# A decoder layer on one core: weight sums handed out one unit later in the plan, and the second down factor split during the last up product

## The chip, the cores and the metric

The kernel runs on one core of a Trainium2 chip. The metric is the device time of one execution in microseconds, measured on that core. The kernel before took a median of 954.35 us over three runs (953.08 to 955.14 us).

## What is computed

One layer of a decoder trunk, for 512 tokens of width 1024, all in float32: retention and dilated attention side by side, their gated sum, a feed-forward block, and a gated embedding. The parts that the change touches are the branch gates and the feed-forward block:

```python
h = rmsnorm(x, g_mix)
z = h @ w_in                                   # the last 2048 columns are the gates gl
gate_r, gate_a = split(sigmoid(gl + b_gate), 2)
x = x + (gate_r * ret_branch + gate_a * att_branch) @ w_o
u = rmsnorm(x, g_mlp) @ w_up                   # 1024 -> 4096
x = x + square(relu(u)) @ w_down               # 4096 -> 1024
```

## The kernel before

**Precision.** Every matrix product is made of three TensorE matmuls (lines 262 to 264, `mm3`): each float32 factor is split into a high part, a copy that ScalarE rounds, and a low part, the difference that VectorE forms. For weights the two instructions are in `split_unit`: the copy to `whi` at line 250 and the subtraction to `wlo` at line 251. For activations they are in `slots`: lines 1300 (copy) and 1301 (subtraction) to a tile `f`.

**Seven products.** Large products are done with seven half-size products in place of eight. Product 1 uses the weight block B11, product 5 uses T1, product 2 uses B21, product 3 uses B22, products 6, 7 and 4 use T2, T3 and T4. T1 is the sum of two blocks of weights, one of which is B11 (stored with the sign that the scheme wants). A product has two halves along its contraction, and one half of one weight block is a *unit*: a 128x1024 float32 tile, loaded in one transfer of 512 KB, split once, and read by 24 matmuls of 256 columns (up and gate products, where the weights are the stationary side) or 12 matmuls of 512 columns (down products). `HALVES` gives the order of units for gates, up and down products; it has 12 entries and 14 units:

```python
SEVEN = ((1, 0), (5, 0), (1, 1), (5, 1), (2, 0), (3, 0), (3, 1), (6, 0), (6, 1), (2, 1), (7, None), (4, None))
HALVES = ((1, 0), (1, 1), (5, 0), (5, 1)) + SEVEN[4:]
```

So in `HALVES` units 0 and 1 are B11, units 2 and 3 are T1, unit 4 is the first half of B21, units 5 and 6 are B22, units 7 and 8 are T2, unit 9 is the second half of B21, 10 and 11 are T3, 12 and 13 are T4.

**The plan of weights.** `make_plan` lists all units of the kernel in order. `plan_seven` adds the fourteen of one product. With "T1" in `vector`, T1's raw tile is loaded with one of its two blocks, and VectorE adds B11's raw tile to it (line 226); this is noted in `self.added` under the unit at which it is to be handed out. T2, T3 and T4 reuse a raw tile of an earlier unit: as soon as that unit is split, GpSimd issues an accumulating transfer into it (line 228), noted in `self.chained`. `ahead` walks the plan: it fetches a unit (line 212, on SP), splits it, then does the sum and the accumulating transfer noted under it. `units` is called before each product or half and runs `ahead` two units past what it hands out (`AHEAD`), three in the stages with a fixed order, until the first result of the stage sets it back to two. There are six raw tiles, and four tiles each for `whi` and `wlo`.

**Order on the engines.** In most of the kernel the tile framework's scheduler orders the instructions of each engine from their dependencies and the order in which the program traces them. Inside `manual_schedule` (the product with `w_o`, and everything from the last down product on) ScalarE and VectorE keep the traced order of the instructions inside.

**Feed-forward.** The loop at the end of `tail` runs four times: `up_products` (1024 columns of `w_up`) and then `seven_gemm` on 1024 rows of `w_down`, seven products each. When an up product has ended, `after` evacuates it (line 1323), combines it with an earlier one (line 1325), applies relu and square on ScalarE (lines 1326 and 1327) and forms the seven left factors of the down product: differences on VectorE (lines 1332, 1334 and 1306), then a split (lines 1300 and 1301) in two parts, p = 0 and p = 1. Factors 1 and 5 are split in `after`; the splits of the others are put in the dictionary `before` under the entry of the down product's `HALVES` ahead of which they are traced. The down product's results are added to the residual `x` on VectorE (line 1286).

Of the kernel before, what the change touches and what calls it, by code (L numbers as in the profile page):

```python
# [36 lines left out]
HALVES = ((1, 0), (1, 1), (5, 0), (5, 1)) + SEVEN[4:]  # L37
# [38 lines left out]
def R(ap):  # L76
    return ap.bitcast(F32R)


class Block:  # L80
# [90 lines left out]
    def plan_seven(self, w, r0, c1, c2, order, vector=()):  # L171

        cols = (c1, c2)
        q = lambda i, j, u: w[r0 + 512 * i + 256 * u : r0 + 512 * i + 256 * (u + 1), cols[j] : cols[j] + 512]
        n = len(self.plan)
        units = [(FACTOR[m], v) for m, u in order for v in ((0, 1) if u is None else (u,))]
        at = lambda name, u: n + units.index((name, u))
        for name, u in units:
            if name == "T1":
                src = q(0, 1, u) if name in vector else (q(0, 1, u), q(0, 0, u))  # L180
                if name in vector:
                    self.added[at("B11", u)] = at("T1", u), at("B11", u)
            elif name == "T4" and name in vector:
                self.added[max(at("B21", u), at("T2", u))] = at("T2", u), at("B21", u)
                src = (None, at("T2", u))
            elif name[0] == "B":
                src = q(int(name[1]) - 1, int(name[2]) - 1, u)
            else:
                prev, ij = {"T2": ("T1", (1, 1)), "T3": ("B22", (0, 1)), "T4": ("T2", (1, 0))}[name]
                k = at(prev, u)  # L190
                self.chained[k] = q(*ij, u)
                src = (None, k)
            self.plan.append((src, None))
# [1114 lines left out]
    def up_products(self, h2):  # L1308

        nc = self.nc  # L1310
        U, split = self.slots()
        held, before = {}, {}
        v = lambda ap: ap.rearrange("p (k t) -> p k t", k=2)

        def after(m, p, ps):
            k = slice(2 * p, 2 * p + 2)
            if m in (1, 3, 5):
                held[m, p] = self.tmp("r") if m != 5 else self.tabp.tile([P, 512], F32, tag="tab", name=self.nm("r5"))
                nc.scalar.activation(held[m, p], ps, AF.Copy)
                return  # L1320
            x = self.tmp("r4") if m == 4 else held[{2: 1, 6: 3, 7: 5}[m], p]
            if m == 4:
                nc.scalar.activation(x, ps, AF.Relu)
            else:
                nc.vector.tensor_tensor(x, x, ps, op=ALU.add)
                nc.scalar.activation(x, x, AF.Relu, scale=1.0 if m == 2 else -1.0)
            nc.scalar.activation(x, x, AF.Square)
            a11, a12, a21 = held.get((3, p)), held[1, p], held[5, p]
            if m == 6:
                split(1, v(a11), k)  # L1330
            elif m == 7:
                nc.vector.tensor_tensor(a11, a11, a21, op=ALU.subtract)
            elif m == 4:
                nc.vector.tensor_tensor(a21, x, a21, op=ALU.subtract)
                split(5, v(a21), k)
                self.differ(a21, x, a11)
                s3 = self.tmp("r3")
                rest = lambda m, a: lambda: split(m, v(a), k)
                third = lambda: self.differ(s3, a12, a21)
                for i, fn in ((p, third), (5 * p, rest(2, a12)), (1 + p, rest(3, s3)), (4 + p, rest(6, a21)),  # L1340
                              (7 + p, rest(7, a11)), (9 + p, rest(4, x))):
                    before.setdefault(i, []).append(fn)

        self.seven_products(lambda m, kk: (R(h2[m][:, 0, kk]), R(h2[m][:, 1, kk])), after, HALVES, "cb")
        return U, before


# [169 lines left out]
```

## Time and profile before

| | |
|---|---|
| median of three runs | 954.35 us (953.08 to 955.14) |
| the profiled execution | 955.36 us |
| its span, first to last instruction | 953.6 us |
| TensorE busy | 943.3 us (99%), 5357 matmuls |
| VectorE busy | 718.4 us (75%) |
| ScalarE busy | 562.1 us (59%) |
| GpSimd busy | 159.5 us (17%) |
| mean granted clock of TensorE | 0.997 |

The profile is of one execution. PE is TensorE's matmul, PEld its weight load, DVE is VectorE, ACT is ScalarE, POOL is GpSimd, SP is SyncE; L251 is line 251 of the kernel. Times run from the start of the span. The end of a matmul is modelled, so its start times are the firmer ones. Releasers are inferred from semaphores. The four up products begin near 587, 665, 744 and 822 us and the four down products near 627, 706, 784 and 863 us.

### The profile page before, as it was taken

The numbers are of one execution on the slowest core, as the hardware profiler recorded it, in microseconds if no ns is written. First come the engines' busy times: TensorE is split into PE (matmuls) and PEld (weight loads), VectorE is DVE, ScalarE is ACT, GpSimd is POOL, SyncE is SP. The second block draws the span as 40 slices with busy tenths as digits, with TensorE's granted clock in tenths as the row PEclk, the third lists the DMA queues.
The fourth block names the chain that finished last, engine by engine and source line by source line (L and its number), as shares of the span: only waits on it lengthen the run. The fifth ranks groups of instructions, "written<-read, shape, count | busy, mean of one in ns | idle before, by whom it ended". The sixth has DMA issues, their size and how long they took to land.

```text
span 953.6 us, 14325 instructions
## 1 busy us (share of the span) xinstructions
PE 943.3 (99%) x5357; PEld 826.2 (87%) x5357; DVE 718.4 (75%) x997; ACT 562.1 (59%) x1065; POOL 159.5 (17%) x140
## 2 busy tenths in 40 slices
PE   9999999999899999999999999999999999999998
PEld 6888888888788888999988888988998998998887
DVE  7789964766697849386937889799499689769953
ACT  5657775445745566576714446884494486467651
POOL 0322210222001112223012211111212302112100
PEclk9999999999999999999999999999999999999999
DMA  9953466258437645869737677868958968876911
GB/s 333 282 170 82 106 141 215 64 118 195 148 111 155 173 100 138 163 181 217 232 115 236 148 178 214 206 153 222 199 156 202 191 183 157 224 172 159 288 50 56
DMA packets 92549, 162.87 MB, mean 171 GB/s; under 512 B 8608, under 2 KB 20544, under 8 KB 92480
## 3 DMA queue, kind: packets, MB, share of 16 engines
q1 hardware_dynamic: 65168, 113.37, 36.4%
q0 software_dynamic: 23936, 46.14, 29.0%
q10 hardware_dynamic: 3376, 2.44, 0.9%
q8 instruction: 42, 0.69, 0.3%
q14 instruction: 27, 0.22, 0.1%
HBM read 153.49 MB, written 6.34 MB: 168 GB/s over the span
## 4 chain that ended last, share of the span: by engine, by line
PE 92%; DVE 3%; ACT 1%; issue 1%; DMA 1%; POOL 1%; SPq 0%; ACTq 0%; POOLq 0%; DVEq 0%
PE pg L264 25%; PE pg L262 25%; PE pg L263 25%; PE pa L264 3%; PE pa L263 3%; PE pa L262 3%; PE po L835 1%; PE ph L590 1%; DVE wlo L251 1%; PE pe L694 1%; PE sc L787 1%; PE ry L1083 1%; PE kv L1070 1%; PE ry L1085 1%; DVE ro L578 0%
## 5 line engine op out<-in xcount | busy, mean ns | idle before, releaser
L251 DVE TENSOR_TENSOR wlo<-raw,whi 128x1024 fp32r<-128x1024 f32 (+1 forms) x258 | 306.8, 1198 | 112.7 <-ACT whi L250 111.8
L250 ACT ACTIVATE whi<-raw 128x1024 fp32r<-128x1024 f32 (+1 forms) x257 | 266.3, 1041 | 212.1 <-PE pg L264 87.2
L263 PE MATMUL pg<-f,whi 128*128 128x256 f32 x384 | 108.7, 283 | 0.0
L264 PE MATMUL pg<-f,wlo 128*128 128x256 f32 x384 | 108.7, 283 | 0.0
L262 PE MATMUL pg<-f,whi 128*128 128x256 f32 x384 | 108.7, 283 | 0.0
L262 PE MATMUL pg<-whi,hh 128*128 128x512 f32 x248 | 98.6, 398 | 0.0
L264 PE MATMUL pg<-whi,hl 128*128 128x512 f32 x248 | 97.1, 392 | 0.0
L263 PE MATMUL pg<-wlo,hh 128*128 128x512 f32 x248 | 96.8, 390 | 0.0
L262 PE MATMUL pg<-whi,f 128*128 128x512 f32 x192 | 75.4, 393 | 0.0
L263 PE MATMUL pg<-wlo,f 128*128 128x512 f32 x192 | 74.8, 389 | 0.0
L264 PE MATMUL pg<-whi,f 128*128 128x512 f32 x192 | 74.8, 389 | 0.0
L262 PEld LDWEIGHTS pg<-f,whi 128*128 128x128 f32 x384 | 73.7, 192 | 0.2
L263 PEld LDWEIGHTS pg<-f,whi 128*128 128x128 f32 x384 | 73.7, 192 | 0.2
L264 PEld LDWEIGHTS pg<-f,wlo 128*128 128x128 f32 x384 | 73.7, 192 | 0.0
L228 POOL DMA_DIRECT2D raw<-in_w_in x32 | 38.9, 1216 | 197.8 <-DVE wlo L251 193.0
L264 PEld LDWEIGHTS pg<-whi,hl 128*128 128x128 f32 x248 | 46.6, 188 | 9.8
L263 PEld LDWEIGHTS pg<-wlo,hh 128*128 128x128 f32 x248 | 46.6, 188 | 9.2
L262 PEld LDWEIGHTS pg<-whi,hh 128*128 128x128 f32 x248 | 46.6, 188 | 9.2
L228 POOL DMA_DIRECT2D raw<-in_w_down x24 | 29.0, 1215 | 139.3 <-DVE wlo L251 108.2
L262 PE MATMUL pg<-whi,us 128*128 128x512 f32 x128 | 52.1, 407 | 0.0
L228 POOL DMA_DIRECT2D raw<-in_w_up x24 | 29.0, 1211 | 135.0 <-DVE wlo L251 124.7
L264 PE MATMUL pg<-whi,us 128*128 128x512 f32 x128 | 50.0, 391 | 0.0
(280 smaller groups left out, 2298.0 us busy)
## 6 DMA issues: line engine op xcount, KB each, us to landing
raw<-in_w_in SPq DMA_DIRECT2D x72, 512.0 KB, 4.1
raw<-in_w_in POOLq DMA_DIRECT2D x32, 512.0 KB, 6.2
raw<-in_w_up SPq DMA_DIRECT2D x32, 512.0 KB, 4.6
raw<-in_w_down SPq DMA_DIRECT2D x32, 512.0 KB, 4.6
raw<-in_w_up POOLq DMA_DIRECT2D x24, 512.0 KB, 6.6
raw<-in_w_down POOLq DMA_DIRECT2D x24, 512.0 KB, 5.9
x<-in_x SPq DMA_DIRECT2D x8, 512.0 KB, 8.2
raw<-in_w_ret_out SPq DMA_DIRECT2D x8, 512.0 KB, 3.8
```

The lines of the kernel that those rows point to most:

```text
L228: self.nc.gpsimd.dma_start(raw, self.chained[i].rearrange("(k p) n -> p k n", p=P), accum_op=ALU.add)
L250: self.pin(nc.scalar.activation(R(hi[:, i]), raw[:, i], AF.Copy))
L251: nc.vector.tensor_tensor(R(lo[:, i]), raw[:, i], hi[:, i], op=ALU.subtract)
L262: t.matmul(ps, sh, mh, start=first, stop=False, skip_group_check=more)
L263: t.matmul(ps, sh, ml, start=False, stop=False, skip_group_check=more)
L264: t.matmul(ps, sl, mh, start=False, stop=last, skip_group_check=more)
L590: self.nc.tensor.transpose(ps[:, t * P : (t + 1) * P], rots[t][:, h * HD : (h + 1) * HD], self.ident)
L694: self.nc.tensor.transpose(ps[:, k * P : (k + 1) * P], e[:, k * P : (k + 1) * P], self.ident)
L787: nc.tensor.matmul(sc[:, h * P : (h + 1) * P], qT[:, h, rs], kT[:, h, rs], start=True, stop=True)
L835: nc.tensor.matmul(po[:, h * P : (h + 1) * P], v[:, vt, h * HD : (h + 1) * HD], pt, start=b == 0, stop=b == len(blocks) - 1)
L1070: nc.tensor.matmul(ps, kd[:, n, hs], v[:, n, c], start=True, stop=True)
L1083: nc.tensor.matmul(y, sT[0][:, r], v[:, i, c], start=True, stop=i == 0)
```

## The change

In `plan_seven`, the vector sum of T1 is noted under the unit ahead of T1's own, no longer under B11's. With `HALVES` the sum for unit 2 is then handed out after unit 1 is split (before: after unit 0), and the sum for unit 3 after unit 2 is split (before: after unit 1). With `SEVEN` the unit ahead of T1's is B11's, and nothing changes.

In `up_products`, the split of the second left factor of the following down product leaves `before` (entries 0 and 5 of the down product) and is traced ahead of entry 11 of the up product, its last one, through a new dictionary `own` that is handed to `seven_products`.

```diff
@@ -179,7 +179,7 @@
             if name == "T1":
                 src = q(0, 1, u) if name in vector else (q(0, 1, u), q(0, 0, u))
                 if name in vector:
-                    self.added[at("B11", u)] = at("T1", u), at("B11", u)
+                    self.added[at("T1", u) - 1] = at("T1", u), at("B11", u)
@@ -1309,7 +1309,7 @@
         U, split = self.slots()
-        held, before = {}, {}
+        held, before, own = {}, {}, {}
@@ -1326,7 +1326,9 @@
             a11, a12, a21 = held.get((3, p)), held[1, p], held[5, p]
-            if m == 6:
+            if m == 2:
+                own.setdefault(11, []).append(lambda: split(2, v(x), k))
+            elif m == 6:
                 split(1, v(a11), k)
@@ -1337,11 +1339,11 @@
-                for i, fn in ((p, third), (5 * p, rest(2, a12)), (1 + p, rest(3, s3)), (4 + p, rest(6, a21)),
+                for i, fn in ((p, third), (1 + p, rest(3, s3)), (4 + p, rest(6, a21)),
                               (7 + p, rest(7, a11)), (9 + p, rest(4, x))):
                     before.setdefault(i, []).append(fn)
 
-        self.seven_products(lambda m, kk: (R(h2[m][:, 0, kk]), R(h2[m][:, 1, kk])), after, HALVES, "cb")
+        self.seven_products(lambda m, kk: (R(h2[m][:, 0, kk]), R(h2[m][:, 1, kk])), after, HALVES, "cb", own)
         return U, before
```

## Rows read from the trace of the kernel before

**Rows 1.** The page, busy time (share of span) and instructions of each engine

```profile
PE 943.3 (99%) x5357; PEld 826.2 (87%) x5357; DVE 718.4 (75%) x997; ACT 562.1 (59%) x1065; POOL 159.5 (17%) x140
```

**Rows 2.** Waits of PE, whole span: total us, times, longest

```profile
PE pc L884 <- DVE wide L878: 3.0, 1, 3.0
...
PE sc L795 <- DVE sm L678: 0.8, 1, 0.8
```

**Rows 3.** Stretches: length, busy us (count) by engine, clock, DMA share, GB/s

```profile
665.00:706.00 41.00, 41.00 (x340) 40.88 (x340) 26.74 (x29) 27.07 (x38) 7.25 (x6) 1.00 0.77 184
706.00:744.00 38.00, 38.00 (x168) 31.05 (x168) 36.80 (x47) 21.40 (x28) 7.25 (x6) 1.00 0.82 190
863.00:903.00 40.00, 40.00 (x187) 32.90 (x186) 38.69 (x55) 26.91 (x43) 8.83 (x8) 1.00 0.84 210
587.00:903.00 316.00, 316.00 (x2036) 288.72 (x2035) 262.69 (x320) 205.98 (x291) 59.61 (x50) 1.00 0.82 193
```

**Rows 4.** Waits of TensorE's weight loads from 587 to 930 us

```profile
PEld pg L262 <- DVE x L1286: 0.3, 1, 0.3
```

**Rows 5.** Line 226 (ns min/median/max); the page's DMA issues of down weights

```profile
L226 DVE TENSOR_TENSOR raw<-raw,raw x32: 1214/1218/1227, 56.9 to 854.8; 128x1024 f32<-128x1024 f32 x32
...
raw<-in_w_down SPq DMA_DIRECT2D x32, 512.0 KB, 4.6
```

**Rows 6.** Timeline (start, us, what), second gate product: VectorE, then TensorE

```profile
423.75 2.35 DVE L251 TENSOR_TENSOR wlo<-raw,whi 128x1024 fp32r<-128x1024 f32 x2
...
427.99 0.36 PE L262 MATMUL pg<-hh,whi 128*128 128x256 f32 x1
```

**Rows 7.** Timeline of VectorE, last up to last down product

```profile
854.82 1.22 DVE L226 TENSOR_TENSOR raw<-raw,raw 128x1024 f32<-128x1024 f32 x1
...
862.01 0.69 DVE L1334 TENSOR_TENSOR r<-r,r 128x512 f32<-128x512 f32 x1 [0.17 <-ACT r L1327]
863.40 0.69 DVE L1301 TENSOR_TENSOR f<-r,f 128x512 fp32r<-128x512 f32 x1 [0.70 <-ACT f L1300]
...
865.46 0.68 DVE L1301 TENSOR_TENSOR f<-r,f 128x512 fp32r<-128x512 f32 x1
...
866.66 1.22 DVE L251 TENSOR_TENSOR wlo<-raw,whi 128x1024 fp32r<-128x1024 f32 x1
...
875.53 1.40 DVE L1286 SCALAR_TENSOR_TENSOR x<-pg,f,x 128x512 f32<-128x512 f32 x2
...
879.79 2.35 DVE L251 TENSOR_TENSOR wlo<-raw,whi 128x1024 fp32r<-128x1024 f32 x2
```

**Rows 8.** Timeline of VectorE, second up to second down product

```profile
706.81 1.28 DVE L1301 TENSOR_TENSOR f<-r,f 128x512 fp32r<-128x512 f32 x2
...
714.68 2.35 DVE L251 TENSOR_TENSOR wlo<-raw,whi 128x1024 fp32r<-128x1024 f32 x2
...
720.61 0.68 DVE L1301 TENSOR_TENSOR f<-r,f 128x512 fp32r<-128x512 f32 x1
```

**Rows 9.** Timeline of TensorE: unit 4 (second down); units 2, 5 (last)

```profile
716.74 0.39 PE L263 MATMUL pa<-wlo,f 128*128 128x512 f32 x1
...
868.40 0.39 PE L263 MATMUL pg<-wlo,f 128*128 128x512 f32 x1
...
876.42 0.47 PE L262 MATMUL pg<-whi,f 128*128 128x512 f32 x1
```

**Rows 10.** Timeline of ScalarE, last up to last down product

```profile
860.73 0.58 ACT L1323 ACTIVATE r<-pg 128x512 f32<-128x512 f32 x1
...
862.73 1.15 ACT L1300 ACTIVATE f<-r 128x512 fp32r<-128x512 f32 x2 [0.76 <-DVE r L1334]
...
877.20 1.06 ACT L250 ACTIVATE whi<-raw 128x1024 fp32r<-128x1024 f32 x1 [0.70 <-DMA raw<-in_w_down]
```

**Rows 11.** Stretches behind the two waits of TensorE, columns as in rows 3

```profile
110.00:120.00 10.00, 10.00 (x50) 8.36 (x49) 8.52 (x18) 9.50 (x30) 1.20 (x1) 1.00 0.69 150
256.00:260.00 4.00, 3.89 (x16) 3.09 (x17) 0.00 (x0) 4.00 (x15) 0.00 (x0) 0.59 0.64 244
```

## The prediction

> **What bounds the kernel now.** I read four views in this order. First the busy shares of the page: TensorE is busy for 943.3 of 953.6 us, VectorE for 718.4 and ScalarE for 562.1 [rows 1]. A busy TensorE may still be one that waits inside modelled ends, so second comes what TensorE waited for: over the whole kernel there are two waits of note, 3.0 us for `wide` (line 878) and 0.8 us for `sm` (line 678) [rows 2], both long before the stages that this change touches. The third view is the busy time by stage. From 587 to 903 us, which is nearly all of the four up and down products, TensorE is busy for every one of 316 us; the only wait of its weight loads there that concerns this change is 0.3 us on VectorE's update of `x` (line 1286) [rows 3, 4]. An up product (665 to 706) has VectorE at 26.7 of 41 us; a down product (706 to 744) has it at 36.8 of 38, and the last one (863 to 903) at 38.7 of 40 [rows 3]. So the time is TensorE's, and VectorE is full just where an up product hands over to a down product. The fourth view is the order of time on VectorE and ScalarE at that hand-over, set against the matmul that first needs each result. I call the difference the lead. A lead above zero costs nothing; VectorE's order matters only where a lead is small.
>
> **What can be won.** Only waits of TensorE can be given back, and in the stages touched these come to the 0.3 us of [rows 4]. That is the whole of the gain side.
>
> **The sums.** Ten plans use the order HALVES with a vector sum (two gate products, four up, four down), so 20 of the 32 instructions of line 226 move; the twelve of the other order stay, since there the unit before T1's is B11's own. Each takes 1.218 us [rows 5], 24.4 us in all, none added or removed. Each is traced one unit later than before, just ahead of the split that reads it (a unit is 2.7 us of TensorE in a down and 2.9 in an up product: 38 and 41 us over 14 units [rows 3]). Where the scheduler orders VectorE it may still pull a sum forward, because it depends only on two landed loads. In the gate products the narrowest lead is that of the second one's first unit: its subtraction, the first of two from 423.75, ends 1.2 us later, and its matmul starts at 427.99 [rows 6]. 3.0 us of lead hide one sum of 1.2 us. The raw tile of B11 is released one unit later, so the load on SP that takes its buffer goes out about 2.8 us later and lands a median of 4.6 us after that [rows 5]. The unit that it feeds is the seventh, five units (some 13 us) behind, so I cost this at nothing; without that cover it would be 2.8 us.
>
> **The last down product is different.** There VectorE and ScalarE keep the written order. Before, both sums come with units 0 and 1, inside the last up product, the second at 854.82. Now the second sum is written between the splits of units 2 and 3, inside the fixed order. From 863.40 until past 875.53 VectorE shows no idle time [rows 7], so what goes in pushes all behind it: unit 3's copy on ScalarE (which reads the sum) and the copies behind that, the subtractions of units 3 and 4, and the updates of `x` after the first two matrices. A 128x1024 instruction in a full queue adds 1.13 us (two take 2.35, one 1.22 [rows 7, 8]). Out of the stretch goes the subtraction of the second factor's first part (line 1301, at 865.46), which adds 0.60 (two take 1.28, one 0.68 [rows 7, 8]). Net: +0.53 us. The first reader with no lead is unit 5: it accumulates onto the bank that the updates from 875.53 read; the first of that pair of 1.40 us ends near 876.3, and TensorE's matmul starts at 876.42 [rows 7, 9]. This is the place of the 0.3 us of [rows 4], so 0.53 us of delay there is 0.53 us of the end time. On the way, unit 2 has 0.5 us (866.66 + 1.22 = 867.88 against 868.40 [rows 7, 9]), and the sum now stands behind it. POOL queues the load that is added onto unit 3's raw tile behind unit 3's subtraction; ScalarE's copy at 877.20 already stands 0.70 us for its landing [rows 10]. It becomes late by the same amount, and its subtraction is the second of the pair from 879.79, near 880.9 [rows 7]: 2.7 us after that copy's end at 878.26, which hides it.
>
> **The second factor.** Its two parts per down product (two copies, 1.15 us back to back on ScalarE [rows 10], and two subtractions, 1.28 us on VectorE; 9.7 us in four products) come ahead of the last up matrix instead of at down units 0 and 5. No DMA moves with them; the tile is taken from its pool one matrix earlier. Behind the copies on ScalarE stands the relu of the last up matrix (line 1323, at 860.73), whose square releases VectorE's line 1334 at 862.01 and, through the copies from 862.73, line 1301 at 863.40 [rows 7, 10]. If both push that chain, 1.15 us are added ahead of VectorE's full stretch: 0.53 + 1.15 = 1.68 us. If the scheduler finds room for both, 0. The trace does not show which. The row at 860.73 has no idle time before it, so ScalarE had no room just there; I take the middle, 0.6.
>
> In the first three down products unit 4 has the least lead: its subtraction, the first of a pair from 714.68, ends at 715.90, and its matmul starts at 716.74 [rows 8, 9]: 0.84 us (0.99 and 0.81 in the two others of this pattern). The second factor's second part I place at 720.61 before, behind that pair, as its position at unit 5 says [rows 8]; now it stands ahead: 0.60 us of 0.84, hidden with about 0.2 us to spare. Bounds: 0, and with ScalarE's delay in full 0.60 + 1.15 - 0.84 = 0.9 us in each.
>
> **The sum.** Last down product 0.53 + 0.6 = 1.1 us; first three 0; gates 0; gain taken as 0. The profiled execution took 955.36 us (span 953.6), above the highest of the three timed runs (953.08 to 955.14, median 954.35). So 956.5 on its scale, and on the median's 954.35 + 1.1 = 955.4 us. About 0.2%, 1.9 us, is what a measurement of this kernel can tell from no change.
>
> **Rivals.** *Hidden anyway:* the scheduler already ran sums and factor when their data was ready, so nothing moves but the one sum, which finds room, and the 0.3 us of [rows 4] may vanish. For it: the factor's first part already ran ahead of unit 2 [rows 7]. Against it: in the last product the order is written out. Time 954.0 to 954.6, say 954.2; chance 0.27. *Unit 4 is overrun (slower):* from the point where more than 0.84 us is put ahead of it, each of three products pays, up to 0.9, and the last 1.68: 4.4 at most. Half of the three, 1.4, with 1.1 gives 2.5: 956.9; chance 0.15. For it: VectorE is at 36.8 of 38 us [rows 3]. Against it: only 0.60 us is certain to move there. *Faster by over 0.2%* would need 1.9 us of waits where the rows hold 0.3: 0.03.
>
> *TensorE's clock falls behind a wait*, inside the 0.15: after the 3.0 us wait at `wide` the granted clock was 0.59 over 256 to 260, a mixture of its levels 1.2 and 2.4 GHz, so (1 - 0.59) x 4 = 1.6 us were lost; after the 0.8 us wait it was 1.00 over 110 to 120 [rows 2, 11]. The waits I expect, near 1 us, are nearer to the second, so I add nothing; with it my forecast would be 957.0. The Trainium skill, TensorE: Matmul & The Clock Gate, What's actually happening, says that an idle array falls to half clock and that only activity releases it; by that rule every new wait has a second price, and the row at `wide` agrees, while the one at `sm` shows none.
>
> **How the numbers follow.** Forecast 0.55 (954.9 to 956.0, from +0.53 to +1.68), hidden 0.27, slower 0.15, faster 0.03. The range takes in the hidden case less 1 us of spread between runs, and the slower case somewhat past its middle: 953.2 to 957.4. Within 0.2% lie forecast and hidden, 0.82; slower 0.15; faster 0.03.
>
> **What would show it.** In the changed kernel the window 863 to 903 holds one instruction of line 226 (none before), the update of `x` after the second matrix ends about 1 us later against the start of that product, and the wait on line 1286 grows from 0.3 to more than 1 us. The three earlier down products show no wait of TensorE. If the wait does not grow, copies and sum found room; if TensorE waits for `wlo` at a unit 4, the slower rival holds. A new wait in the gate products, or a shift before them, would make this account wrong.

## The result and the profile after

The changed kernel takes a median of 959.00 us (956.70 to 962.62, six runs), against 953.72 us for the kernel before in its six runs: 5.3 us longer, ratio 1.0065, 95% interval 1.0042 to 1.0088. The forecast was 955.4 us, its range ended at 957.4. The change makes this kernel slower.

The profiled execution of the changed kernel took 957.49 us (span 955.4 us), the second shortest of the six. Its waits of TensorE (us in all, times, longest), the view of [rows 2]; the two left out, 1.4 and 0.3 us, stand in the view of the kernel before with the same length:

```profile
...
PE pg L262 <- DVE x L1286: 1.4, 2, 0.9
PE pg L262 <- ACT pp L533: 1.4, 1, 1.4
PE pc L884 <- DVE wide L878: 0.7, 1, 0.7
PE pg L262 <- DVE r L1325: 0.7, 1, 0.7
PE sc L795 <- DVE sm L678: 0.6, 1, 0.6
PE pg L263 <- DVE wlo L251: 0.5, 1, 0.5
PE pg L262 <- ACT whi L250: 0.5, 1, 0.5
...
```

Its stretches, columns as in [rows 3]:

```profile
564.00:580.00 16.00, 14.59 (x72) 11.62 (x71) 13.88 (x16) 6.75 (x9) 0.00 (x0) 1.00 0.36 122
863.00:903.00 40.00, 38.49 (x175) 30.75 (x174) 37.50 (x51) 24.71 (x39) 8.27 (x7) 1.00 0.82 204
587.00:903.00 316.00, 312.77 (x2002) 284.25 (x2001) 258.96 (x314) 202.44 (x287) 57.88 (x48) 1.00 0.80 189
```

And the first of these stretches in the kernel before:

```profile
564.00:580.00 16.00, 15.84 (x78) 12.80 (x77) 14.57 (x19) 7.17 (x11) 0.00 (x0) 1.00 0.41 132
```

From 587 to 903 us TensorE was never idle before [rows 3]; now it idles for 3.2 us (316.00 - 312.77). From 564 to 580, a stretch that the prediction did not look at, another 1.25 us are lost (15.84 - 14.59). The wait at `wide`, in code that the change does not touch, happens to be 0.7 us here and 3.0 us in [rows 2], so these two spans show less than the difference of the medians. Four of the new waits, at 576.59, 816.31, 871.66 and 877.42 us, turned out to be the change's own; each is followed below. The one on line 1325 is not, and a second, shorter one on line 1286, at 899.14 us, is not followed.

### The profile page after: what moved, and what is told of

Read it like the earlier page. It is cut to its first block, busy times and chain, and to the rows that moved or that the text cites. A ratio compares the mean times of both kernels' runs of the same rounds, so it can differ in the third digit from the quotient of the medians.

```text
span 955.4 us, 14326 instructions
## 1 busy us (share of the span) xinstructions
PE 943.2 (99%) x5357; PEld 824.2 (86%) x5357; DVE 719.0 (75%) x997; ACT 561.4 (59%) x1065; POOL 159.5 (17%) x140
## 4 chain that ended last, share of the span: by engine, by line
PE 84%; DVE 6%; DMA 3%; issue 3%; ACT 2%; POOL 1%; SPq 0%; ACTq 0%; POOLq 0%; DVEq 0%
PE pg L262 23%; PE pg L263 23%; PE pg L264 23%; PE pa L264 3%; PE pa L263 3%; PE pa L262 3%; DVE wlo L251 2%; DMA raw<-in_w_down 2%; PE po L835 1%; PE ph L590 1%; ACT whi L250 1%; PE sc L787 1%; PE ry L1083 1%; PE pe L694 1%; DMA raw<-in_w_in 1%
```

## Experiments

All were run in five rounds beside the kernel before. A ratio is to that kernel, with its 95% interval; 0.001 is 0.95 us. The edits move lines down by up to six: L252 and L257 of an experiment are line 251 of the kernel before, L1288 and L1292 are line 1286.

**The two halves of the change.** One kernel has the first hunk of the diff alone (the sums), one has the rest (the second factor).

> Only the sums move (line 182); the second factor is split where it was. The changed kernel takes 5.3 us more than before, by the medians. Theory 'sums': the sums carry nearly all of it, because the one in the first up product leaves the fixed order and the one in the last down product enters it; 4 to 5.5 us more than before, ratio 1.004 to 1.006, with TensorE waits of 1.4 us near 575 us and about 2 us in the last down product. Theory 'factor': the second factor, put ahead of the last up matrix, delays the evacuations (line 1325) of that product; then this kernel is within 1 us of before, ratio up to 1.001. Theory 'both needed': 2 to 3 us.

Measured: 958.51 us, ratio 1.0042 (1.0025 to 1.0058).

> Only the second factor moves; the sums are handed out as before. Theory 'sums': 0 to 1 us more than before, ratio below 1.001, no new TensorE wait over 0.5 us in the last down product. Theory 'factor': 4 to 5.5 us more, with waits at the start of the fourteenth product entry of each up product. The forecast's own step for this part was 0.6 us, in the last down product.

Measured: 955.39 us, ratio 1.0009 (0.9998 to 1.0019). The sums, which the prediction costed at 0.53 us (1.13 for the sum that enters the full stretch, less 0.60 for the factor's part that leaves it), are by far the larger part, some 4 us.

**Which sums.** The changed kernel, but with the sums of the first up product and of the last down product handed out as before:

```diff
+                    self.added[at("T1", u) - 1 if self.late else at("B11", u)] = at("T1", u), at("B11", u)
...
+            self.late = f > 0
             self.plan_seven(a["w_up"][0], 0, 1024 * f + 512, 1024 * f, HALVES, ("T1",))
+            self.late = f < 3
             self.plan_seven(a["w_down"][0], 1024 * f, 512, 0, HALVES, ("T1",))
```

> The changed kernel, but with the sums of the first up product and of the last down product handed out as before (the two plans whose sums stand at an edge of the fixed order); the other eight plans keep the change, and the second factor too. Theory 'edges': the waits near 575 us (1.4) and in the last down product (1.6 to 2.3) go, so 3 to 3.7 us of the 5.3 come back: 1.5 to 2.3 us over before, ratio 1.002. Theory 'loads': the later release of B11's raw tile bunches the loads in every product, and the edges matter little: still 4 us or more over before.

Measured: 955.55 us, ratio 1.0021 (1.0008 to 1.0033). More than half of the loss is gone with 4 of 20 sums. The other way round, the kernel before with `late` set for one group of sums only. In the first up product (`f == 0`):

> The kernel before, with the new hand-out of sums in the first up product alone. Theory 'edges': its first sum is no longer inside the fixed order of the stage of w_o, the scheduler puts it some 16 us earlier on VectorE, between the differences that the left factors need, and TensorE waits 1.4 us for an evacuation of the embedding's product near 575 us: 1 to 1.5 us over before, ratio 1.001 to 1.0015. Theory 'loads': no change, within 0.5 us.

Measured: 956.03 us, ratio 1.0022 (1.0010 to 1.0035). In the last down product (`f == 3`):

> The kernel before, with the new hand-out of sums in the last down product alone. Theory 'fixed order': the second sum then stands between the splits of units 2 and 3 on VectorE, TensorE waits about 0.8 to 1 us for unit 3's low part and 0.6 to 0.8 us behind the second matrix: 1.5 to 2 us over before, ratio 1.0015 to 1.002 (my forecast's own step for the sum alone was 0.53 us). Theory 'loads': nothing, below 0.5 us.

Measured: 955.89 us, ratio 1.0030 (1.0018 to 1.0041). In the up products 2 to 4 and the down products 1 to 3:

> Before, with the new hand-out of the sums only in the second, third and fourth up products and the first three down products (12 of the 20 sums); the second factor as before. The prediction put these at nothing: ratio 0.9993 to 1.0007. Rival 'narrow leads' (a sum that waits for its own load stands on VectorE ahead of the evacuation that frees product 4's bank, lead 0.3 to 0.5 us, or of an update of x): 0.5 to 1.7 us, ratio 1.0005 to 1.0018, with waits of TensorE at the start of product 4 near 697 and 776 us or inside a down product.

Measured: 953.45 us, ratio 0.9997 (0.9987 to 1.0008). In the gates:

> Before, with the new hand-out of the sums only in the two gate products; all else as before. The prediction put these at nothing, with a lead of 3.0 us at the narrowest place: ratio 0.999 to 1.001, about 953.3. Rival 'late load' (the raw tile of the first block comes free one unit later, and the load that takes it lands too late): 1 us or more, ratio 1.001 to 1.003, with a wait of TensorE for a weight split between 360 and 450 us.

Measured: 953.26 us, ratio 0.9995 (0.9985 to 1.0005). So 16 of the 20 sums cost nothing, as predicted, and four cost some 2.1 and 2.9 us. With the factor's 0.9 that is 5.9 us, and the measured total is 5.3 us by the medians, 6.2 us (4.0 to 8.4) by the ratio: nothing large is missing.

**The first up product.** VectorE after and before, near 565 to 585 us (start, us, what, idle time before it and its releaser):

```profile
564.80 0.68 DVE L524 TENSOR_TENSOR plo<-pl,ph 128x512 fp32r<-128x512 f32 x1
565.67 1.22 DVE L226 TENSOR_TENSOR raw<-raw,raw 128x1024 f32<-128x1024 f32 x1 [0.18 <-DMA raw<-in_w_up]
566.81 0.68 DVE L524 TENSOR_TENSOR plo<-pl,ph 128x512 fp32r<-128x512 f32 x1
...
572.79 1.23 DVE L1371 TENSOR_TENSOR zq<-zq,zq 128x1024 f32<-128x1024 f32 x1
...
581.44 1.22 DVE L226 TENSOR_TENSOR raw<-raw,raw 128x1024 f32<-128x1024 f32 x1
```

```profile
569.11 1.28 DVE L524 TENSOR_TENSOR plo<-pl,ph 128x512 fp32r<-128x512 f32 x2
...
581.57 1.22 DVE L226 TENSOR_TENSOR raw<-raw,raw 128x1024 f32<-128x1024 f32 x1
...
584.44 1.22 DVE L226 TENSOR_TENSOR raw<-raw,raw 128x1024 f32<-128x1024 f32 x1
```

Before, the two sums ran 12.5 and 15.3 us after the first of the two instructions of line 524. Now one of them stands between these two: handed out "one unit later", it runs earlier. It is the second sum, that of unit 3: it starts 0.13 us after the landing of the fourth load of `w_up`, at 565.54, while the first one, of unit 2, runs at 581.44, right behind the split of unit 1 where it was handed out. The stage with `w_o` ends with a call of `units` that splits two units ahead, units 0 and 1 of the first up product. Before, both sums were noted under these two and so stood in the stage's fixed order. Now the sum of unit 3 is noted under unit 2, which is traced after that stage, where the scheduler may place it anywhere; it depends on two loads alone and went ahead. (The expectation of the first-up-product experiment took it for the first sum.) What follows on VectorE is pushed by about one such instruction. ScalarE and TensorE, after:

```profile
574.05 1.06 ACT L1300 ACTIVATE f<-zq 128x1024 fp32r<-128x1024 f32 x1 [7.86 <-DVE zq L1371]
...
575.96 1.55 ACT L533 ACTIVATE pp<-pg 128x512 f32<-128x512 f32 x3
...
576.59 0.50 PE L262 MATMUL pg<-whi,ph 128*128 128x512 f32 x1 [1.41 <-ACT pp L533]
```

and before:

```profile
576.95 1.06 ACT L1300 ACTIVATE f<-zq 128x1024 fp32r<-128x1024 f32 x1 [6.45 <-DVE zq L1369]
...
579.49 0.50 PE L262 MATMUL pg<-whi,ph 128*128 128x512 f32 x1 [0.16 <-ACT pp L533]
```

ScalarE stands 7.86 us in place of 6.45 for the difference `zq`; the evacuation of `pp` is queued behind that, and TensorE needs the bank: 0.16 us of wait become 1.41 (1.40 in the kernel with this hand-out alone, so the trace shows 1.2 of the 2.1 us; the rest lies within the interval, 1.0 to 3.3). To test this, the two sums of the kernel with the new hand-out in the first up product alone were tied to the traced order:

```diff
-                self.nc.vector.tensor_tensor(total, total, part, op=ALU.add)
+                ins = self.nc.vector.tensor_tensor(total, total, part, op=ALU.add)
+                if i in self.fixed:
+                    self.tc.keep_in_program_order(ins)
...
```

> As the first-up-product experiment (new hand-out of its sums alone), but each of these two sums is tied behind the instruction traced ahead of it on VectorE, so that the scheduler can't put it earlier. Theory 'pulled forward': the 1.4 us wait near 575 us goes and the kernel is back within 0.7 us of before (953 to 954.5). Theory 'handed out late': the sum comes late for the split of unit 2 and the 1.0022 stays.

Measured: 953.52 us, ratio 1.0002 (0.9992 to 1.0012), and the second sum on VectorE is late again, with the row of TensorE as before:

```profile
585.15 1.22 DVE L230 TENSOR_TENSOR raw<-raw,raw 128x1024 f32<-128x1024 f32 x1
...
576.74 0.50 PE L268 MATMUL pg<-whi,ph 128*128 128x512 f32 x1 [0.16 <-ACT pp L539]
```

The 2.1 us are gone, with both sums behind the splits that they now follow. Not the later place cost them but the freedom to be early.

**The last down product.** VectorE, ScalarE and TensorE after, at units 2 and 3:

```profile
866.30 1.22 DVE L251 TENSOR_TENSOR wlo<-raw,whi 128x1024 fp32r<-128x1024 f32 x1
...
868.04 1.22 DVE L226 TENSOR_TENSOR raw<-raw,raw 128x1024 f32<-128x1024 f32 x1
869.17 0.69 DVE L1306 SCALAR_TENSOR_TENSOR r<-r,r 128x512 f32<-128x512 f32 x1
870.38 1.22 DVE L251 TENSOR_TENSOR wlo<-raw,whi 128x1024 fp32r<-128x1024 f32 x1 [0.53 <-ACT whi L250]
...
869.29 1.06 ACT L250 ACTIVATE whi<-raw 128x1024 fp32r<-128x1024 f32 x1 [2.84 <-DVE raw L226]
...
871.66 0.50 PE L263 MATMUL pg<-wlo,f 128*128 128x512 f32 x1 [0.53 <-DVE wlo L251]
...
877.42 0.97 PE L262 MATMUL pg<-whi,f 128*128 128x512 f32 x3 [0.49 <-ACT whi L250]
```

Before, the subtraction of unit 3 ran at

```profile
868.40 1.22 DVE L251 TENSOR_TENSOR wlo<-raw,whi 128x1024 fp32r<-128x1024 f32 x1
```

and TensorE read it at 871.12, 1.5 us after its end. Now sum, copy and subtraction of unit 3 stand one behind the other (868.04, 869.29, 870.38, end 871.60: 3.6 us). ScalarE, which had made that copy ahead, stands 2.84 us for the sum, and VectorE, for which the prediction counted on a queue without gaps, stands 0.53 us for the copy. The difference of line 1306 (869.17) also stands ahead of that subtraction now; before, it came behind it, at 869.53. The prediction had only the push of 0.53 us at unit 5. To tell a push from a chain, the next kernel leaves both sums where they were and adds, at the new place of the second one, an addition of the same size that nothing reads:

```diff
+            if i in self.dummy:
+                part = self.raws[self.dummy[i]][0]
+                self.nc.vector.tensor_tensor(part, part, part, op=ALU.add)
...
```

> Before, with the last down product's two sums where they were, and one more 128x1024 addition on VectorE that nothing reads (the first block's raw tile added to itself, after its split) at the place where the changed kernel has its second sum: after the split of unit 2 of the last down product, inside the fixed order. VectorE's full stretch is 1.2 us longer, as with the sum alone in the last down product (2.65 us, ratio 1.003), but no copy on ScalarE waits for it. Theory 'serial chain' (the moved sum costs because sum, copy and subtraction of unit 3 now stand one behind the other, about 3.6 us, where copy and sum had been done ahead): the spare addition costs only its push on the first update of x, 0.3 to 1.1 us, 953.6 to 954.5 on a before of 953.3, ratio 1.0003 to 1.0012, with no wait for unit 3's split. Rival 'full queue' (1.2 us of work more in a full stretch is all that counts): the same 2.0 to 2.9 us as the moved sum, ratio 1.002 to 1.003.

Measured: 954.72 us, ratio 1.0012 (1.0002 to 1.0022). VectorE there, the spare addition in the second line, then ScalarE and TensorE:

```profile
863.72 1.22 DVE L257 TENSOR_TENSOR wlo<-raw,whi 128x1024 fp32r<-128x1024 f32 x1
...
865.46 1.22 DVE L232 TENSOR_TENSOR raw<-raw 128x1024 f32<-128x1024 f32 x1
866.59 0.68 DVE L1312 SCALAR_TENSOR_TENSOR r<-r,r 128x512 f32<-128x512 f32 x1
867.19 1.22 DVE L257 TENSOR_TENSOR wlo<-raw,whi 128x1024 fp32r<-128x1024 f32 x1
...
862.79 1.05 ACT L256 ACTIVATE whi<-raw 128x1024 fp32r<-128x1024 f32 x1
...
868.47 0.50 PE L269 MATMUL pg<-wlo,f 128*128 128x512 f32 x1
...
874.61 0.47 PE L268 MATMUL pg<-whi,f 128*128 128x512 f32 x1 [0.64 <-DVE x L1292]
```

VectorE has no gap, ScalarE makes the copy of unit 3 ahead (862.79), and one wait is listed, that of unit 5 on the update of `x`. Unit 3 is only just in time: its first matmul with the low part (868.47) starts 0.06 us after the subtraction ends (867.19 + 1.22 = 868.41), and 0.95 us after the last one of unit 2 in place of 0.68. So the push, with the difference that moved ahead of the subtraction (line 1312 here), has used up the 1.5 us of unit 3's lead by itself. With the real sum in the last down product alone, the same views show three:

```profile
868.25 1.06 ACT L251 ACTIVATE whi<-raw 128x1024 fp32r<-128x1024 f32 x1 [2.24 <-DVE raw L227]
...
866.53 0.50 PE L264 MATMUL pg<-wlo,f 128*128 128x512 f32 x1 [0.29 <-DVE wlo L252]
870.62 0.50 PE L264 MATMUL pg<-wlo,f 128*128 128x512 f32 x1 [0.76 <-DVE wlo L252]
...
876.77 0.47 PE L263 MATMUL pg<-whi,f 128*128 128x512 f32 x1 [0.60 <-DVE x L1288]
```

The wait of 0.29 us is unit 2's, whose subtraction stands ahead of the moved sum, so it is not the chain's: in this execution the subtraction of line 1301 with which VectorE's full stretch begins came 1.61 us after TensorE's first matmul of the product, against 0.70 before and 0.67 with the spare addition. The kernel with all sums moved, whose code in this product is the same, had 0.88 us and no wait at unit 2, and still shows

```profile
872.98 0.50 PE L263 MATMUL pg<-wlo,f 128*128 128x512 f32 x1 [0.77 <-DVE wlo L251]
...
879.13 0.47 PE L262 MATMUL pg<-whi,f 128*128 128x512 f32 x1 [0.64 <-DVE x L1286]
```

So by the times the push costs about 1.1 us and the real sum 2.9. What only the chain has is VectorE's wait of 0.53 us for the copy; how much of the rest is the chain's and how much a late start like that of this execution is not shown. The two intervals just overlap; what separates the cases is that unit 3's low part is waited for by 0.5 to 0.8 us with the real sum in three kernels, and by no listed wait with the spare one. The traces give a second measure, the time from the first matmul of the last down product to the end of the span (before: 953.6 - 862.70), one execution each:

| kernel | us |
|---|---|
| before | 90.9 |
| new sums in the first up product, the same tied, in the gates, in the middle products | 90.9 to 91.0 |
| spare addition | 92.2 |
| all sums moved; those of the last down product alone | 93.0; 93.8 |
| factor moved in the first three products | 90.7 |
| factor moved in all four; the same with the 16 other sums moved | 91.8; 91.7 |
| changed | 93.2 |

By it the push costs 1.3 us, the real sum 2.1 to 2.9, and the changed kernel loses 2.3 us here.

**The second factor.** The factor moved in the first three products only, the sums as before:

> The second factor moved as in the change, but only ahead of the first three down products; sums as before. Theory 'fixed order': the second factor's cost (0.9 us alone) lies in the last product, where the chain of the last up matrix starts VectorE's full stretch late; here 0 to 0.4 us over before. Theory 'fifth unit': it lies in the first three and 0.6 us or more stay.

Measured: 953.82 us, ratio 1.0014 (1.0002 to 1.0027); with all four products it was 1.0009. By the medians it is 0.6 us here and 1.7 with all four. So the times don't tell in which products the factor costs; the traces show both places. In the last product the kernel with the factor alone (sums as before) has, on VectorE and then TensorE,

```profile
863.03 0.69 DVE L1301 TENSOR_TENSOR f<-r,f 128x512 fp32r<-128x512 f32 x1 [1.60 <-ACT f L1300]
...
866.85 0.50 PE L263 MATMUL pg<-wlo,f 128*128 128x512 f32 x1 [0.60 <-DVE wlo L251]
```

The copy that releases line 1301 stands on ScalarE behind two copies of weights, VectorE's full stretch starts late, and TensorE waits 0.60 us for the low part of unit 2. The kernel with the factor in all four products and the old sums in this one has the same wait, 0.59 us; the one with the factor in three has none, and by the table above the difference is 1.0 to 1.1 us. In the first three products no wait for `wlo` stands at a unit 4. VectorE and TensorE near the end of the third down product, before and then in this kernel:

```profile
815.40 0.74 DVE L1286 SCALAR_TENSOR_TENSOR x<-pg,f,x 128x512 f32<-128x512 f32 x1
816.06 1.21 DVE L226 TENSOR_TENSOR raw<-raw,raw 128x1024 f32<-128x1024 f32 x1
```

```profile
813.60 1.22 DVE L226 TENSOR_TENSOR raw<-raw,raw 128x1024 f32<-128x1024 f32 x1
814.73 0.74 DVE L1286 SCALAR_TENSOR_TENSOR x<-pg,f,x 128x512 f32<-128x512 f32 x1
815.39 1.21 DVE L226 TENSOR_TENSOR raw<-raw,raw 128x1024 f32<-128x1024 f32 x1
...
815.62 0.47 PE L262 MATMUL pg<-whi,f 128*128 128x512 f32 x1 [0.63 <-DVE x L1286]
```

With the factor moved, the scheduler places a sum of the next up product ahead of the update of `x` that frees a bank; TensorE waits 0.63 us for it here, and 0.95 in the changed kernel at 816.31, where the order is the same. In the kernel with the factor alone the order is this one too, with 0.2 us of wait.

**Are the sums better late?** A last theory was that the sums stand too early in the queue of VectorE. In this kernel all sums of up and down products keep the old hand-out but are tied behind the split they follow in the trace:

> The kernel before, with the sums of all up and down products tied behind the split traced ahead of them (hand-out as before). Theory 'queue': in each up product VectorE stands 0.5 to 2 us on the load of T1's first half, ahead of the evacuation of product 7, whose bank product 4 needs within 0.3 to 0.5 us; with the sum behind the splits that idle time goes and TensorE doesn't wait at product 4 in any run: 0.5 to 1.5 us below before, ratio 0.9985 to 0.9995, with a smaller spread. Theory 'slack': those waits are none in the kernel before and nothing changes (within 0.3 us).

Measured: 957.38 us, ratio 1.0043 (1.0032 to 1.0055). The theory falls. Of its waits of TensorE, 2.5 us between 587 and 905 us, the largest group is

```profile
PE pa L268 <- DVE wlo L256: 1.5, 3, 0.5
```

These are three waits of 0.5 us at 636 to 797 us, one in each of the first three down products, at unit 4: the place with 0.84 us of lead in the prediction's second rival. The tie moved neighbours of the sums too, so this shows that the lead there is narrow, not the price of the sums' order alone.

**A wait that is not the change's.** The wait of 0.7 us on line 1325 in the changed kernel (a bank of product 7 that product 4 of an up product takes) invites a story: a sum that stands for its own load is queued ahead of the evacuation. The order is as this story has it: before and after the change that evacuation starts 4.08 us after the sum. But in the kernel with late sums in the gates only, whose up products are those of before and whose ratio is 0.9995, the same view has

```profile
PE pg L263 <- DVE r L1327: 1.4, 3, 0.6
```

(line 1325 moved by two). That kernel's profiled execution, 954.60 us, was one of the two longest of its twelve, whose median is 953.26. So this wait comes and goes between executions, and is not the change's.

## Why the prediction was wrong

- **What bounds the kernel, and the gain side: right.** TensorE was full (the view of [rows 2] has a third wait, 1.4 us at the kernel's start, which the prediction leaves out; it is 1.4 us in every kernel here), and no variant is measurably below the kernel before: the lowest ratio, 0.9995, has an interval that holds 1.
- **Gates and middle products: right.** 16 sums at nothing, measured 0.9995 and 0.9997. The load that goes out later [rows 5, 6] is hidden.
- **"Where the scheduler orders VectorE it may still pull a sum forward": the step that failed.** It was named and left at nothing, with leads read in the gates and the down products only. The first up product's second sum leaves a fixed order, so the freedom was new there, and what it was pulled in front of belongs to the stage before, which the prediction did not read. Size: 2.1 us (1.0 to 3.3) where the sum had 0; the result lies 1.6 us above the range. Tied to its place, the sum costs nothing.
- **The last down product: right in place, too small in size, and the second step that failed.** The sum entered the fixed order and pushed unit 5 as foreseen: 1.13 us forecast for the push, about 1.1 measured with a spare addition. What was missing is the sum's own reader: "unit 3's copy on ScalarE (which reads the sum)" was counted as pushed by 0.5 us, when it stood 2.84 us, and VectorE then stood 0.53 us for it. I gave the leads of units 2 and 5 and not that of unit 3, 1.5 us; the sum and the difference that now stands ahead used it up, and the gap came on top. In all 2.9 us (1.7 to 3.9) for the sum alone, where the terms of the prediction give 1.13.
- **The second factor: fair in the last product, too low in the first three.** 0.6 us forecast in the last product, and the traces show 0.8 to 0.9 there, with a wait of 0.6 at unit 2. In the first three, put at 0, unit 4 held as forecast, and 0.2 to 0.95 us were lost at the end of the third, through an order of VectorE that changed some 30 us behind the edit. The measured total, 0.9 us (-0.2 to 1.8), doesn't tell these apart.
- **The rivals.** *Hidden anyway* fell. *Unit 4 is overrun* had the sign and came nearer in time (956.9), by a mechanism that the changed kernel does not show. *The clock falls behind a wait* fell: behind waits of up to 1.41 us the granted clock is 1.00 in each of the stretches above. The Trainium skill, TensorE: Matmul & The Clock Gate, What's actually happening, has the array at half clock when it has been idle and at full clock when it has been active. The prediction read from it a second price on every new wait, which is more than it says: by the row at `wide` [rows 11] a wait of 3.0 us had one, by these rows waits of up to 1.41 us had none.
- **The test that was set.** One instruction of line 226 in 863 to 903, as said. The wait on line 1286 was to pass 1 us at unit 5; it was 0.5, and named the copy. "The three earlier down products show no wait of TensorE" failed: the third has one of 0.95 us. The last sign, a new wait in the gate products or a shift before them, did not come; the loss at 576 us lies behind the gates, where the prediction had set no sign.

## What to carry to other kernels

Where instructions can be reordered, handing one out later is no promise that it runs later: ask first whether the edit takes it out of an order that held it, and read the stage in front of that edge as well. Where an instruction enters a full, ordered queue, cost it twice: as a push on all behind it, and as the head of its own chain through the other engines, against the lead of its own reader. A wait in one trace is the change's only if kernels without that part of the change do not show it. And where totals can't tell two parts apart, the length of one stage, compared between the traces of all kernels that change it and that don't, may.

## What was not expected of the hardware

The same 512 KB load takes quite different times to land. The first half of T1's block in the first down product took 6.9 us before, 7.9 in the changed kernel, and in the three later down products 4.2 to 4.7; VectorE stood 0.5 to 1.6 us for it with the sum at the head of its queue. Waits that hang on such landings, as that on line 1325, differ between runs of like code by as much as a small edit is worth.
